# An attention loop's items nine steps deep instead of ten, its group-norm steps turned by half an iteration

## The chip, the core and the metric

The kernel runs on one core of a Trainium2 chip. The metric is device time in microseconds (us) of one execution, on the slowest (here the only) core. The engines are TensorE (PE; its weight loads are shown as PEld), VectorE (DVE), ScalarE (ACT), GpSimd (POOL) and SyncE (SP), which only issues transfers. Each engine takes its own instructions in order, and waits for other engines by semaphores.

## The reference

One encoder block over 1024 tokens of width 1024, in float32. The part that matters here is the middle of it:

```python
h = rms_norm(x, norm_mix_g)
(na_q, na_k, na_v, p_r, p_k, p_v, ..., mem_q, gate_na, gate_rw, gate_mem) = split_columns(h @ w_in)
y_na  = neighborhood_attention(na_q, na_k, na_v, na_rpb)     # 6 heads, windows of 8 x 16 in a 16 x 64 grid
y_rw  = rwkv7_bidirectional(...)                             # two scans, then a group norm per head, x gate
y_mem = memory_attention(mem_q, rms_norm(mem), w_mem_kv)     # 4 heads over 256 memory rows
merged = sigmoid(gate_na) * (y_na @ w_branch_na) + sigmoid(gate_rw) * (y_rw @ w_branch_rw) \
       + sigmoid(gate_mem) * (y_mem @ w_branch_mem)
x = x + merged @ w_out
x = x + expert_choice_ffn(rms_norm(x), ...)                  # 16 experts
```

Both attentions are a softmax over scores times values. The group norm of the scan's output is `((y - mean) * rsqrt(var + eps)) * ln_g + ln_b`, over the 64 channels of a head, plus a bonus, times a gate `sigmoid(lat_g) @ g2`.

## The kernel before

The program is a row of stages: projections and scans, then the **attention stage** (with its tail 843 to 999.6 us of the profiled span), then the merge of the branches, the output projection, the router, and the experts, which take the second half of the span.

The attention stage is an order written out by hand (`tc.manual_schedule()`), a loop over n. It handles 40 items: 24 of the neighbourhood attention (`na_item`, two heads and one eighth of the tokens each) and then 16 of the memory attention (`mem_item`). Each item is cut into parts, and `PIPE` says how many iterations after its start each part is issued, latest part first in an iteration. So iteration n issues lo of item n-9, hi of item n-8, and so on down to score of item n. The parts, with their engines:

- score (PE), top (DVE: bias, maximum), exp (ACT), trans (DVE reciprocal; PE transposes of the probabilities to PSUM tile `tr`), evac (ACT and DVE copy `tr` to `pt`; POOL spreads the reciprocals over `rq`);
- mix (PE: `pt` times values into one half of the PSUM bank `av`, then a transpose of `rq` into the same half), spread (DVE copies that transpose to `rb`), mul (DVE: `av` times `rb` gives `y`), hi (ACT rounds `y` into `yh`), lo (POOL writes the rest to `yl`).

The two halves of `av` take turns, but they are one tile, so mix waits for the last DVE instruction before it that reads `av`. `y` has 3 buffers, `rb` 2.

Between the items runs the group norm (`group_norm`), a generator over 6 tiles of 128 x 512 with 14 steps each. Each iteration from n = 2 on takes two steps: one behind the parts of `PIPE`, and one behind the loads of the next head pair (`side`: `na_load`, `mem_load`, whose steps split q and k into a rounded value and a rest). The steps of one tile, with the lines of the profile of before:

- POOL adds the scans (L876, L877), PE takes off the mean ("cent", L884), ACT copies and squares (L886, L887), PE sums the squares ("hsel", L891), DVE and POOL form the reciprocal root (L210, L211), ACT spreads it (L898), PE transposes it ("pb", L902), DVE multiplies (L904), ACT scales (L906), POOL adds the bonus (L907), PE computes the gate ("pg", L909), DVE multiplies (L913), ACT and POOL write `yh` and `yl` (L916, L917).

All four PE results go through one PSUM tile `gn` with one buffer. When the loop ends, the first weights of the merge (`wraw`, L1127) are loaded over the space of the group norm's tiles.

Of the kernel before, what the change touches and what calls it, by code (L numbers as in the profile page):

```python
# [25 lines left out]
F32 = mybir.dt.float32  # L26
# [4 lines left out]
OP = mybir.AluOpType  # L31
# [22 lines left out]
GN0 = 2  # L54
SCB = 1
WB0, WBK = 2, 4
PIPE = (("lo", 9), ("hi", 8), ("mul", 7), ("spread", 6), ("mix", 5), ("evac", 4), ("trans", 3), ("exp", 2), ("top", 1), ("score", 0))
NB_ = dict(s=2, tr=2, gn=1, av=1)
PSEQ = "E A | B X | x0 | r0 | s0 o0 x1 | r1 | s1 o1 L | | T"
PRI, XTB = None, 3  # L60
# [100 lines left out]
def block_kernel(ctx: ExitStack, tc: tile.TileContext, T, out, dbg=None, upto=99):  # L161
    nc = tc.nc
    dbg = dbg or {}
    V, A, G, PE, SP = nc.vector, nc.scalar, nc.gpsimd, nc.tensor, nc.sync
# [122 lines left out]
    with tc.tile_pool(name="wp", bufs=1, side="right", reuse_waits="tile") as wp:  # L287
# [14 lines left out]
        with (tc.tile_pool(name="qp", bufs=1, side="right", reuse_waits="tile") as qp,  # L302
# [64 lines left out]
            for j in range(3):  # L367
# [13 lines left out]
                for d in range(2):  # L381
# [7 lines left out]
                    rb = qp.tile([128, 8, 2, 64], F32, name="rb", bufs=1)  # L389
# [379 lines left out]

    yctx = ExitStack()  # L770
    ap = yctx.enter_context(tc.tile_pool(name="ap_", bufs=1, side="right", reuse_waits="tile"))
    for nm, w, n in (("sb", 768, 4), ("pt", 768, 2), ("y", 128, 3), ("rb", 128, 2), ("rq", 128, 2)):
        ap.tile([128, w] if w == 128 and nm != "rq" else [128, 2, w // 2], F32, name=nm, bufs=n)
    na, bias = {}, {}
    grid = lambda t: t.rearrange("p (r c) -> p r c", c=64)
# [77 lines left out]
    def group_norm():  # L853
        g2 = gq.tile([128, 384], F32, name="g2")
        SP.dma_start(g2, T["g2"])
        lg = gq.tile([128, S], F32, name="lg")
        SP.dma_start(lg, plat[0])
        its = [(t0, j) for t0 in (0, 512) for j in range(3)]
        ld = {}

        def load(n):
            if n < len(its):
                t0, j = its[n]
                ld[n] = []
                for nm, src in (("y0", yrw[0]), ("y1", yrw[1]), ("b0", bon[0]), ("b1", bon[1])):
                    t = gq.tile([128, 512], F32, name=nm, bufs=2)
                    SP.dma_start(t, src[j][:, t0:t0 + 512])
                    ld[n].append(t)

        load(0)  # L870
        yield
        yield
        for n, (t0, j) in enumerate(its):
            load(n + 1)
            y0, y1, b0, b1 = ld.pop(n)
            G.tensor_tensor(y0, y0, y1, op=OP.add)  # L876
            G.tensor_tensor(b0, b0, b1, op=OP.add)  # L877
            if n == 0:
                A.activation(lg, lg, AF.Tanh, scale=0.5)
                G.tensor_scalar(lg, lg, 0.5, 0.5, op0=OP.mult, op1=OP.add)  # L880
            yield
            yield
            pcb = abank("gn")
            PE.matmul(pcb, C("cent"), y0, start=True, stop=True)  # L884
            yield
            A.activation(y1, pcb, AF.Copy)  # L886
            A.activation(b1, pcb, AF.Square)  # L887
            yield
            pn = abank("gn")
            for i in range(4):  # L890
                PE.matmul(pn[:, 2 * i:2 * i + 2], b1[:, i * 128:(i + 1) * 128], C("hsel"), start=True, stop=True)  # L891
            yield
            rn = gq.tile([128, 8], F32, name="grn", bufs=2)
            rinv_of(pn[:, 0:8], rn, 8, 1.0 / 64, 64e-5)
            rb = gq.tile([128, 8, 64], F32, name="grb", bufs=1)
            yield
            yield
            A.activation(rb, rn[:, :, None].to_broadcast([128, 8, 64]), AF.Copy)  # L898
            yield
            pb = abank("gn")  # L900
            for i in range(4):
                PE.transpose(pb[:, i * 128:(i + 1) * 128], rb[:, 2 * i:2 * i + 2].rearrange("p h t -> p (h t)"), ident)  # L902
            yield
            V.tensor_mul(y1, y1, pb)  # L904
            yield
            A.activation(y1, y1, AF.Identity, bias=P_("lnb", j), scale=P_("lng", j))  # L906
            G.tensor_tensor(y1, y1, b0, op=OP.add)  # L907
            pg = abank("gn")
            PE.matmul(pg, g2[:, j * 128:(j + 1) * 128], lg[:, t0:t0 + 512], start=True, stop=True)  # L909
            yield  # L910
            yield
            yield
            V.tensor_mul(y1, pg, y1)  # L913
            yield
            hi = yh[:, 3 + j, t0:t0 + 512]
            A.activation(hi, y1, AF.Copy)  # L916
            G.tensor_tensor(yl[:, 3 + j, t0:t0 + 512], y1, hi.bitcast(F32), op=OP.subtract)  # L917
# [3 lines left out]
    def attention(sign, score_of, top_of, trans_of, evac_of, mix_of, tokens):  # L921
        o = {}

        def score():
            score_of(o)

        def top():
            o["st"] = ap.tile([128, 8], F32, name="st", bufs=6)
            top_of(o)

        def exp():
            for h in range(2):
                A.activation(o["sb"][h], o["e"][h], AF.Exp, bias=o["st"][:, h:h + 1], scale=sign, accum_out=o["st"][:, 4 + h:5 + h])

        def trans():
            V.reciprocal(o["st"][:, 6:8], o["st"][:, 4:6])
            trans_of(o)

        def evac():
            o["pt"] = ap.tile([128, 2, 384], F32, name="pt", bufs=2)  # L940
            evac_of(o)
            o["rq"] = ap.tile([128, 2, 64], F32, name="rq", bufs=2)
            G.tensor_copy(o["rq"], o["st"][:, 6:8, None].to_broadcast([128, 2, 64]))

        def mix():
            turn[0] ^= 256
            o["av"] = av = avs[:, turn[0]:turn[0] + 256]
            mix_of(o, av)
            PE.transpose(av[:, 128:256], o["rq"].rearrange("p h c -> p (h c)"), ident)

        def spread():
            o["rb"] = rb = ap.tile([128, 128], F32, name="rb", bufs=2)
            V.tensor_copy(rb, o["av"][:, 128:256])

        def mul():
            o["y"] = ap.tile([128, 128], F32, name="y", bufs=3)
            V.tensor_mul(o["y"], o["av"][:, 0:128], o["rb"])

        def hi():
            A.activation(tokens(yh), tokens(o["y"]), AF.Copy)  # L960

        def lo():
            G.tensor_tensor(tokens(yl), tokens(o["y"]), tokens(yh).bitcast(F32), op=OP.subtract)

        return locals()
# [51 lines left out]
    def mem_load():  # L1017
        kv = ap.tile([128, S], F32, name="kt", bufs=1).rearrange("p (j m) -> p j m", j=4)
        SP.dma_start(kv, pkv.rearrange("j p t -> p j t"))
        raw = [ap.tile([128, S], F32, name="q", bufs=2) for _ in range(2)]  # L1020
        for j in range(2):
            SP.dma_start(raw[j], pmq[j])
        yield
        yield
        A.activation(kb[0], kv[:, 0:2], AF.Copy, scale=-1.0)
        V.scalar_tensor_tensor(kb[1], kv[:, 0:2], -1.0, kb[0].bitcast(F32), op0=OP.mult, op1=OP.subtract)
        yield
        yield
        yield
        vm = ap.tile([128, 4, 4, 128], F32, name="VT", bufs=2)[:, 0].rearrange("p (m a) t -> p m (a t)", m=2)  # L1030
        vms.append(vm)
        for j in range(2):
            qm.append([ap.tile([128, 2, 4, 128], F32R, name=f"qb{v}", bufs=2).rearrange("p a g t -> p (a g t)") for v in "hl"])
            for v in (slice(0, 512), slice(512, 1024)):
                A.activation(qm[j][0][:, v], raw[j][:, v], AF.Copy)
                G.tensor_tensor(qm[j][1][:, v], raw[j][:, v], qm[j][0][:, v].bitcast(F32), op=OP.subtract)
                yield
            if j == 0:
                p = abank("s")
                for m in range(2):  # L1040
                    for i in range(2):
                        PE.transpose(p[:, m, i * 128:(i + 1) * 128], kv[:, 2 + i, m * 128:(m + 1) * 128], ident)
                yield p, vm, None
# [37 lines left out]
    with tc.manual_schedule():  # L1081
# [6 lines left out]
        side = {0: na_load(1), 8: na_load(2), 16: mem_load()}  # L1088
        gn = group_norm()
        live, extra, pend = {}, [], []  # L1090
        for n in range(len(items) + 10):
            if n in side:
                extra.append(side[n])
            if n < len(items):
                f, a, b = items[n]
                live[n] = f(a, b)
            for part, lag in PIPE:
                if n - lag in live:
                    live[n - lag][part]()
            for v in pend:  # L1100
                v_out(*v)
            pend = []
            if n >= GN0:
                next(gn, 0)
            live.pop(n - 9, None)
            if n in (4, 8, 12):
                bias_load(n // 4 + 2)
            for g in list(extra):
                v = next(g, 0)
                if v == 0:  # L1110
                    extra.remove(g)
                elif v:
                    pend.append(v)
            if n >= GN0:
                next(gn, 0)
# [456 lines left out]
```

## Time and profile before

| what | us |
|---|---|
| median of 3 runs (2352.61 to 2361.06) | 2359.86 |
| the profiled execution | 2365.62 |
| its span | 2363.8 |
| PE busy in the span | 2238.7 (95%) |
| DVE busy | 1665.0 (70%) |
| ACT busy | 1313.0 (56%) |
| POOL busy | 623.9 (26%) |
| attention stage with its tail, 843 to 999.6 | 156.6 |

The mean granted TensorE clock of the span is 0.973 of full speed. The profiled execution is 5.8 us above the median of the runs, and 1.8 us of it lie outside the span. "Idle before" an instruction is time in which its engine waited, and the arrow names what ended the wait.

### The profile page before, as it was taken

The numbers are of one execution on the slowest core, as the hardware profiler recorded it, in microseconds if no ns is written. First come the engines' busy times: TensorE is split into PE (matmuls) and PEld (weight loads), VectorE is DVE, ScalarE is ACT, GpSimd is POOL, SyncE is SP. The second block draws the span as 40 slices with busy tenths as digits, with TensorE's granted clock in tenths as the row PEclk, the third lists the DMA queues.
The fourth block names the chain that finished last, engine by engine and source line by source line (L and its number), as shares of the span: only waits on it lengthen the run. The fifth ranks groups of instructions, "written<-read, shape, count | busy, mean of one in ns | idle before, by whom it ended". The sixth has DMA issues, their size and how long they took to land.

```text
span 2363.8 us, 33505 instructions
## 1 busy us (share of the span) xinstructions
PE 2238.7 (95%) x12494; PEld 1810.1 (77%) x12494; DVE 1665.0 (70%) x2030; ACT 1313.0 (56%) x1588; POOL 623.9 (26%) x1269
## 2 busy tenths in 40 slices
PE   7999999999999989799948999999999999999996
PEld 6777787877877866577837888888888888888885
DVE  6556566556556246563277888888888988898887
ACT  5554234333334356421226777777777777777775
POOL 1000567567666335442040000000000000000001
PEclk9999999999999999799968999999999999999998
DMA  6435444433433362165396999999999999999994
GB/s 229 157 146 201 123 114 121 138 106 110 128 102 101 116 226 72 59 212 172 121 350 251 378 381 379 391 391 385 393 382 379 380 388 390 389 384 390 380 345 197
DMA packets 196499, 594.19 MB, mean 251 GB/s; under 512 B 53360, under 2 KB 100720, under 8 KB 147184
## 3 DMA queue, kind: packets, MB, share of 16 engines
q1 hardware_dynamic: 189280, 566.20, 64.8%
q0 software_dynamic: 5184, 19.73, 3.0%
q10 hardware_dynamic: 1872, 6.13, 0.7%
q8 instruction: 98, 1.61, 0.3%
q14 instruction: 65, 0.53, 0.1%
HBM read 522.61 MB, written 69.39 MB: 250 GB/s over the span
## 4 chain that ended last, share of the span: by engine, by line
PE 51%; DVE 3%; DMA 1%; ACT 1%; POOL 1%; issue 1%; POOLq 0%; ACTq 0%; DVEq 0%
PE y L1439 14%; PE g L1427 5%; PE g L1428 5%; PE g L1430 5%; PE u L1427 5%; PE u L1428 5%; PE u L1430 5%; PE acc L235 2%; PE acc L237 1%; PE acc L236 1%; PE tr L1487 1%; PE tr L1417 1%; POOL m L1172 1%; PE pl L1259 1%; DVE ye L1345 0%
## 5 line engine op out<-in xcount | busy, mean ns | idle before, releaser
L1404 DVE TENSOR_TENSOR ewl<-raw,ewh 128x2048 fp32r<-128x2048 f32 x380 | 849.8, 2284 | 5.5 <-ACT ewh L1399 5.5
L1399 ACT ACTIVATE ewh<-raw 128x2048 fp32r<-128x2048 f32 x380 | 720.8, 1914 | 112.8 <-PE u L1428 82.3
L1446 POOL DMA_INDIRECT acc<-ye,idx x15 | 43.4, 2891 | 949.2 <-DVE ye L1445 872.2
L728 PE MATMUL acc<-hlo,wh 128*128 128x512 f32 x560 | 226.0, 404 | 0.0
L728 PE MATMUL acc<-hhi,wh 128*128 128x512 f32 x560 | 225.7, 403 | 0.0
L728 PE MATMUL acc<-hhi,wl 128*128 128x512 f32 x560 | 225.4, 402 | 0.0
L568 POOL TENSOR_TENSOR tmul<-tinv,blk 96x60 f32<-96x60 f32 (+24 forms) x496 | 174.1, 351 | 147.1 <-DMA blk<-ldr 109.5
L1427 PE MATMUL g<-ewh,xh 128*128 128x512 f32 x512 | 206.1, 403 | 0.0
L1427 PE MATMUL u<-ewh,xh 128*128 128x512 f32 x512 | 202.2, 395 | 0.0
L1428 PE MATMUL g<-ewh,xl 128*128 128x512 f32 x512 | 200.4, 391 | 0.0
L1428 PE MATMUL u<-ewh,xl 128*128 128x512 f32 x512 | 199.5, 390 | 0.0
L570 POOL TENSOR_TENSOR tinv<-tinv,tmul 96x60 f32<-96x60 f32 (+24 forms) x496 | 176.0, 355 | 38.9
L1439 PE MATMUL y<-ewh,ah 128*128 128x512 f32 x512 | 137.9, 391 | 0.7 <-ACT ah L231 0.7
L1439 PE MATMUL y<-ewl,ah 128*128 128x512 f32 x512 | 137.7, 391 | 0.0
L1439 PE MATMUL y<-ewh,al 128*128 128x512 f32 x512 | 137.7, 391 | 0.0
L1430 PE MATMUL g<-ewl,xh 128*128 128x512 f32 x512 | 137.4, 390 | 0.0
L1430 PE MATMUL u<-ewl,xh 128*128 128x512 f32 x512 | 137.0, 389 | 0.0
L728 PEld LDWEIGHTS acc<-hlo,wh 128*128 128x128 f32 x560 | 106.6, 190 | 20.4
L728 PEld LDWEIGHTS acc<-hhi,wl 128*128 128x128 f32 x560 | 106.2, 190 | 20.5
L728 PEld LDWEIGHTS acc<-hhi,wh 128*128 128x128 f32 x560 | 106.2, 190 | 20.3
L231 ACT ACTIVATE ah<-tr 128x512 fp32r<-128x512 f32 x64 | 38.4, 599 | 143.6 <-PE tr L1487 143.6
L232 DVE TENSOR_TENSOR wl<-wraw,wh 128x1024 fp32r<-128x1024 f32 (+1 forms) x60 | 76.0, 1270 | 57.9 <-ACT wh L231 57.9
(319 smaller groups left out, 4365.9 us busy)
## 6 DMA issues: line engine op xcount, KB each, us to landing
raw<-in_wg_dram SPq DMA_DIRECT2D x128, 1024.0 KB
raw<-in_wu_dram SPq DMA_DIRECT2D x128, 1024.0 KB
raw<-in_wd_dram SPq DMA_DIRECT2D x128, 1024.0 KB
wraw<-in_wt_dram SPq DMA_DIRECT2D x46, 512.0 KB
pt<-pz SPq DMA_DIRECT2D x16, 768.0 KB
pgt<-po SPq DMA_DIRECT2D x48, 256.0 KB
gt<-pgt SPq DMA_DIRECT2D x16, 768.0 KB
blk<-ldr SPq DMA_DIRECT2D x64, 96.0 KB
```

The costliest lines, as they stand in the source:

```text
L232: V.tensor_sub(lo, src, hi.bitcast(F32))
L235: PE.matmul(out_, lh, rh, start=(k_ == 0), stop=False)
L568: G.tensor_tensor(tm[:, 0:m, 0:n], tt[:, 0:m, j:j + 1].to_broadcast([4 * NB, m, n]), lt[:, j, None, j + 1:32].to_broadcast([4 * NB, m, n]) ...
L570: G.tensor_tensor(tt[:, 0:m, j + 1:32], tt[:, 0:m, j + 1:32], tm[:, 0:m, 0:n], op=OP.add)
L728: PE.matmul(p, l[:, k], r[:, k, s0:s0 + 512], start=(k == 0 and i == 0), stop=(k == KD - 1 and i == 2))
L1399: A.activation(hi, raws[seq[n]], AF.Copy)
L1404: V.tensor_sub(lo, raws.pop(seq[n]), his[seq[n]].bitcast(F32))
L1427: PE.matmul(p, xh[:, 4 * b + k], wh[:, k], start=(b == 0 and k == 0), stop=False)
L1428: PE.matmul(p, xl[:, 4 * b + k], wh[:, k], start=False, stop=False)
L1430: PE.matmul(p, xh[:, 4 * b + k], wl[:, k], start=False, stop=(b == 1 and k == 3))
L1439: PE.matmul(py[n], l[:, 2 * b + k], r[:, k, n * 512:(n + 1) * 512], start=(f == 0 and b == 0 and i == 0 and k == 0), stop=(f == 3 and b == ...
L1446: G.indirect_dma_start(out=acc[:, :], out_offset=bass.IndirectOffsetOnAxis(ap=idx[:, e:e + 1], axis=0), in_=ye, in_offset=None, compute_op ...
```

## The change

It has five parts. `spread` and `mul` of an item are issued in one iteration (lag 6 for both, spread first), so that hi and lo come one iteration earlier and the loop has one iteration less. `y` gets 6 buffers and `rb` 3. The group norm starts one step later, so that each of its steps falls into the other half of an iteration. Two of the four subtractions that split the memory attention's q (the second half of each tile) go from POOL to DVE. The items are dropped from the table one iteration earlier.

```diff
-PIPE = (("lo", 9), ("hi", 8), ("mul", 7), ("spread", 6), ("mix", 5), ("evac", 4), ("trans", 3), ("exp", 2), ("top", 1), ("score", 0))
+PIPE = (("lo", 8), ("hi", 7), ("spread", 6), ("mul", 6), ("mix", 5), ("evac", 4), ("trans", 3), ("exp", 2), ("top", 1), ("score", 0))
...
-    for nm, w, n in (("sb", 768, 4), ("pt", 768, 2), ("y", 128, 3), ("rb", 128, 2), ("rq", 128, 2)):
+    for nm, w, n in (("sb", 768, 4), ("pt", 768, 2), ("y", 128, 6), ("rb", 128, 3), ("rq", 128, 2)):
...
         load(0)
         yield
         yield
+        yield
         for n, (t0, j) in enumerate(its):
...
-                G.tensor_tensor(qm[j][1][:, v], raw[j][:, v], qm[j][0][:, v].bitcast(F32), op=OP.subtract)
+                (V if v.start else G).tensor_tensor(qm[j][1][:, v], raw[j][:, v], qm[j][0][:, v].bitcast(F32), op=OP.subtract)
...
-        for n in range(len(items) + 10):
+        for n in range(len(items) + 9):
...
-            live.pop(n - 9, None)
+            live.pop(n - 8, None)
```

Lines from 873 on have a number higher by one in the changed kernel. Three places show what moves.

The first is DVE in the fourth tile of the group norm, while memory items run (L957 mul, L953 spread, L1060 top of a memory item, L904 the group norm's first product). Before:

```order
L957 TENSOR_TENSOR y_10066<-av_8761,rb_10032 128x128 [waits DVE_49,PE_49,Pool_49]
L953 COPY rb_10068<-av_8761 128x128
L936 RECIPROCAL st_10008<-st_10008 128x2 [waits Activation_49]
L1060 TENSOR_REDUCE st_10089<-s_10011 128x2 [waits PE_49,Activation_49]
L904 TENSOR_TENSOR y1_9583<-y1_9583,gn_10099 128x512 [waits PE_49]
L957 TENSOR_TENSOR y_10107<-av_8761,rb_10068 128x128 [waits DVE_49,Pool_49]
L953 COPY rb_10109<-av_8761 128x128
```

And now:

```order
L1061 TENSOR_REDUCE st_10092<-s_10013 128x2 [waits PE_49,Activation_49,Pool_49]
L954 COPY rb_10110<-av_8761 128x128 [waits PE_49]
L958 TENSOR_TENSOR y_10112<-av_8761,rb_10110 128x128 [waits DVE_49]
L1072 COPY pt_10119<-tr_10085 128x2x256 [waits PE_49]
L937 RECIPROCAL st_10053<-st_10053 128x2
L1061 TENSOR_REDUCE st_10131<-s_10095 128x2 [waits PE_49,Pool_49]
L905 TENSOR_TENSOR y1_9587<-y1_9587,gn_10103 128x512 [waits PE_49]
```

The group norm's product stands a whole iteration of DVE work later. mul stands behind spread and reads the `rb` just written, so it waits for DVE itself; its wait for POOL (a free `y`) is gone.

The second is ACT at the second tile's cent (L886, L887 read cent's result; L1002 and L933 are evac and exp of the items, L804 and L810 split k and q). Before:

```order
L804 ACTIVATE KTh<-kt 128x512
L886 ACTIVATE y_8875<-gn 128x512 [waits DMAHW4_49,PE_49]
L887 ACTIVATE b_8879<-gn 128x512 [waits DMAHW6_49,Pool_49]
L960 ACTIVATE yh<-y 128x8x16 [waits DVE_49]
L1002 COPY pt<-tr 96x384 [waits Activation_49]
L933 ACTIVATE sb,st<-sb,st 128x384 [waits DVE_49]
```

And now:

```order
L804 ACTIVATE KTh<-kt 128x512
L961 ACTIVATE yh<-y 128x8x16 [waits DVE_49]
L1003 COPY pt<-tr 96x384 [waits PE_49,Activation_49]
L934 ACTIVATE sb,st<-sb,st 128x384 [waits DVE_49,Pool_49]
L934 ACTIVATE sb,st<-sb,st 128x384
L887 ACTIVATE y_8877<-gn 128x512 [waits DMAHW4_49,PE_49]
L888 ACTIVATE b_8881<-gn 128x512 [waits DMAHW6_49,Pool_49]
```

The two readers of `gn` went behind the next iteration's hi, evac and exp; hsel on PE, which needs the square, kept its iteration.

The third is POOL at the start of the second tile (L917 ends the first tile, L876 and L877 begin the second, L805 is the rest of the next k). Before:

```order
L917 TENSOR_TENSOR yl<-y_8842,yh 128x512 [waits Activation_49]
L876 TENSOR_TENSOR y_8873<-y_8873,y_8875 128x512 [waits DMAHW4_49,DMAHW3_49]
L877 TENSOR_TENSOR b_8877<-b_8877,b_8879 128x512 [waits DMAHW6_49,DMAHW5_49]
L805 TENSOR_TENSOR KTl<-kt,KTh 128x512 [waits DMAHW2_49,Activation_49]
L963 TENSOR_TENSOR yl<-y,yh 128x8x16
```

And now:

```order
L805 TENSOR_TENSOR KTl<-kt,KTh 128x512 [waits DMAHW2_49,Activation_49]
L918 TENSOR_TENSOR yl<-y_8842,yh 128x512 [waits Activation_49]
L877 TENSOR_TENSOR y_8875<-y_8875,y_8877 128x512 [waits DMAHW4_49,DMAHW3_49]
L878 TENSOR_TENSOR b_8879<-b_8879,b_8881 128x512 [waits DMAHW6_49,DMAHW5_49]
L964 TENSOR_TENSOR yl<-y,yh 128x8x16
```

The block of three (L917, L876, L877) now stands behind the split of the next k, which waits for a transfer.

## Rows read from the trace of the kernel before

**Rows 1.** Stretches (us from the span's start): busy per engine, granted clock.
```profile
843.00:999.60 156.60, 131.18 (x1037) 91.10 (x1037) 92.73 (x317) 93.90 (x281) 83.47 (x124) 0.86 0.29 100
963.00:973.00 10.00, 8.40 (x49) 6.01 (x48) 5.00 (x15) 5.65 (x19) 4.08 (x10) 0.51 0.00 1
987.00:1004.00 17.00, 12.36 (x47) 7.99 (x48) 6.79 (x17) 6.06 (x14) 6.25 (x13) 0.50 0.43 144
1004.00:1110.00 106.00, 103.03 (x448) 83.10 (x447) 60.45 (x77) 20.31 (x26) 45.60 (x32) 1.00 0.60 198
```

**Rows 2.** PE's waits, 843 to 978.3: line waited for, total us, times, longest.
```profile
PE av L1007 <- DVE rb L953: 6.2, 10, 1.2
PE av L1076 <- DVE rb L953: 4.6, 5, 1.3
```

**Rows 3.** DVE's waits, 843 to 978.3.
```profile
DVE rinv_t L210 <- PE gn L891: 13.8, 5, 4.9
DVE y L904 <- PE gn L902: 11.7, 5, 4.4
DVE y L957 <- POOL yl L963: 10.1, 7, 3.3
```

**Rows 4.** Timeline at the fourth tile's pb: start, duration, engine, line; idle before.
```profile
944.85 0.66 PE L902 MATMUL gn<-cst,grb 128*128 128x128 f32 x4
...
945.55 0.69 DVE L904 TENSOR_TENSOR y<-y,gn 128x512 f32<-128x512 f32 x1 [0.76 <-PE gn L902]
946.15 0.28 DVE L957 TENSOR_TENSOR y<-av,rb 128x128 f32<-128x128 f32 x1
...
946.35 0.28 DVE L953 COPY rb<-av 128x128 f32<-128x128 f32 x1
...
946.78 0.66 PE L1076 MATMUL av<-pt,VT 128*64 128x128 f32 x8 [1.27 <-DVE rb L953]
```

**Rows 5.** Timeline where the fourth tile ends and the fifth begins.
```profile
951.62 0.69 DVE L1060 TENSOR_REDUCE st<-s 128x2 f32<-128x512 f32 x1
...
952.50 0.64 ACT L916 ACTIVATE yh<-y 128x512 fp32r<-128x512 f32 x1
...
953.21 1.27 POOL L917 TENSOR_TENSOR yl<-y,yh 128x512 fp32r<-128x512 f32 x1 [2.28 <-ACT yh L916]
...
955.76 1.12 PE L884 MATMUL gn<-y,cst 128*128 128x512 f32 x2 [0.45 <-POOL y L876]
...
957.37 0.29 DVE L957 TENSOR_TENSOR y<-av,rb 128x128 f32<-128x128 f32 x1 [1.98 <-POOL yl L963]
...
957.92 0.33 PE L1076 MATMUL av<-pt,VT 128*64 128x128 f32 x2 [1.03 <-DVE rb L953]
```

**Rows 6.** Timeline where the third k is split, beside the second tile's cent.
```profile
878.80 0.63 ACT L804 ACTIVATE KTh<-kt 128x512 fp32r<-128x512 f32 x1 [3.47 <-DMA kt<-pna]
...
881.10 1.95 PE L884 MATMUL gn<-y,cst 128*128 128x512 f32 x2
```

**Rows 7.** Timeline: the last instruction of top beside one of POOL.
```profile
903.96 1.28 POOL L917 TENSOR_TENSOR yl<-y,yh 128x512 fp32r<-128x512 f32 x1 [2.19 <-ACT yh L916]
904.00 1.26 DVE L992 TENSOR_SCALAR st<-st 128x2 f32<-128x2 f32 x1
```

**Rows 8.** Timeline of the tail, the last tile of the group norm.
```profile
986.68 0.63 ACT L898 ACTIVATE grb<-grn 128x512 f32<-128x512 f32 x1 [1.22 <-POOL grn L211]
...
987.64 1.12 PE L1076 MATMUL av<-pt,VT 128*64 128x128 f32 x8 [0.91 <-DVE rb L953]
...
989.82 1.06 PE L902 MATMUL gn<-cst,grb 128*128 128x128 f32 x4
...
993.47 1.92 PE L909 MATMUL gn<-lg,g 128*128 128x512 f32 x2
...
999.57 0.80 PE L235 MATMUL acc<-yh,wh 128*128 128x512 f32 x1 [2.73 <-ACT wh L231]
```

**Rows 9.** SP's waits, 840 to 1005.
```profile
SPq L1127 <- PE gn L909: 38.7, 1, 38.7
```

More of the change, by code (lines that the diff above doesn't have):

```diff
@@ L951, in spread @@
         def spread():
-            o["rb"] = rb = ap.tile([128, 128], F32, name="rb", bufs=2)
+            o["rb"] = rb = ap.tile([128, 128], F32, name="rb", bufs=3)
             V.tensor_copy(rb, o["av"][:, 128:256])
         def mul():
-            o["y"] = ap.tile([128, 128], F32, name="y", bufs=3)
+            o["y"] = ap.tile([128, 128], F32, name="y", bufs=6)
             V.tensor_mul(o["y"], o["av"][:, 0:128], o["rb"])
```

## The prediction

> **What bounds the kernel now.** I first cut the span into stretches [rows 1]. The stage that the change touches is 156.6 us long, 6.6% of the span. PE is busy 131.18 us of it, DVE, ACT and POOL some 83 to 94 us each, so PE is the engine that sets its length, and the reader should look at the 25.4 us in which PE is idle. The second number in that row is the granted clock: 0.86. [...] The stretches 963 to 973 and 987 to 1004 show it at 0.51 and 0.50. The stage after it is PE too: 103.03 of 106 us at full clock, so what the attention stage gives back is not lost in the merge.
>
> Next I asked for what PE waits. Up to 978.3, where the loop runs out of scores, mix waits 6.2 + 4.6 = 10.8 us, 15 times, for DVE's spread [rows 2]. Then for what DVE waits, since it is late: the reciprocal root waits 13.8 us for hsel, the first product 11.7 us for pb, mul 10.1 us for POOL's lo [rows 3]. DVE takes its list in order, so what stands behind such a wait is late: spread, and with it the next mix. The timeline shows it whole at one place [rows 4]: pb ends at 945.51, the product starts at 945.55 and takes 0.69, mul and spread follow, and mix starts at 946.78 after 1.27 us of idle PE. The other kind is where one tile ends and the next begins [rows 5]: POOL works through its three long additions, mul waits 1.98 us for a `y` that lo still reads, and PE's mix waits 1.03 us.
>
> **The change part by part.**
>
> *mul beside spread, six `y`, the half iteration.* All three take away reasons for those 10.8 us. With six `y`, mul needs the lo of four iterations ago and waits for no POOL. With the turn, the reciprocal root and both products are issued behind a whole iteration of DVE's item work, and what they read from PE is an iteration old; nothing of the items stands behind a wait for pb or hsel. What stays: mix still waits for the last reader of `av`. That was spread, starting 0.20 behind mul [rows 4] without reading it. Now it is mul, which needs spread's result: 0.28 for spread, and a hand-off of 0.04 (as from pb's end to the product), so 0.32 instead of 0.20: 0.12 more. With the longer hand-off from DVE to PE (spread ends at 946.63, mix starts at 946.78) it would be 0.23, without any 0.08. DVE has the slack for 40 of these; on PE's path I charge it at the 15 places: 1.8. Term: -10.8 + 1.8 = **-9.0**.
>
> *POOL's three long instructions.* ACT's rounding (L916) needs the second product. That product stood in the iteration before; now it is DVE's last work in the same one, behind top. In rows 5: top ends at 952.31, the product 0.69 later at 953.00, ACT's 0.64 then ends at 953.65 instead of 953.14, and POOL starts at 953.7 instead of 953.21. cent waits for POOL already (0.45), so it comes 0.5 later, at tiles three to six: 2.0. Behind the block stands, after lo, the spreading of `rq`, which the next mix's transpose reads; mul no longer waits, but PE may here. Between nothing and the 1.03 that stood there; I take 0.3, nearer to nothing since PE arrives later too: 1.2. Term: **+3.2**.
>
> *The second tile's start.* Here the block also changes places with the split of the next k, which waits 3.47 us for a transfer [rows 6]. ACT's split ends at 879.43 and the rounding at 880.07; POOL's rest of k (1.27 for this size, as L917) runs to 880.8, the block's first two to 883.3. cent ran at 881.10. The transfer does not come earlier because PE does. Term: **+2.2**.
>
> *hsel, pb, pg.* Each now reads what ACT or DVE issues at the end of the same iteration, where it was the iteration before. PE reaches it after mix, transposes and score, and these cover most of it; without cover one operation of this size is 0.6 to 0.69. 18 places less the tail's three, 0.2 each: **+3.0** (0 to 10).
>
> *The two subtractions on DVE* stand at the end of an iteration, 0.69 each as the product of that size, under PE's work; POOL loses 2.5 us just where its block of the fourth tile is. I take 0. A two-column operation of DVE stood 1.26 us beside POOL's L917 and ended with it [rows 7], so the bound is 2 x 1.3 = 2.6 if a subtraction stands likewise and PE is behind it. [...]
>
> *The tail.* After 978.3 the last tile's chain sets the end: ACT has spread its roots by 987.31, but pb runs at 989.82, since the mix ahead of it started at 987.64 after 0.91 of waiting for a spread that stood behind POOL [rows 8]. pb to the gate's matmul L909 is then 3.65 us, with the product ahead of mul on DVE once more. The first weights of the merge are loaded over the group norm's tiles and wait for L909 [rows 9], and the merge starts at 999.57. Without the waits of mul, pb can follow at about 987.5 to 988 (-2), and mix does not stand behind the product (-1.3, as in rows 4); L909 itself, 1.92 here, takes a little over 1 at full clock (as cent's 1.12), -0.7. Term: **-4.0** (0 to -7; the added step of order in each engine is why not more).
>
> *The clock.* [...] In 963 to 973 it is half of 8.40, 4.2. With the long idle places gone some of the drops will not come; others follow the start of the loop and the wait for k, which stay. Rows give only the bounds, and I take **-3**, somewhat less than one such stretch.
>
> **Sum:** -9.0 + 3.2 + 2.2 + 3.0 + 0 - 4.0 - 3 = -7.6. On the profiled execution 2365.6 becomes 2358.0; that one lies 5.8 above the median of the runs, so the median comes to 2352.
>
> **The rivals.**
>
> [...]
> 2. *The waits change places.* cent waits for POOL and the `rq` transpose takes over what mul waited for, hsel and pg cost 0.4 each, the clock stays as it is: -9 + 5 + 2.2 + 6 - 4 = 0, about 2359. For it: POOL's block is as long as before and only starts later.
> 3. *Slower: ACT as the relay.* ACT's scaling (L906) and rounding (L916) of each tile now wait at the end of ACT's list for a product that DVE issues last in the same iteration, and the next iteration's evac, on which the transposes wait, stands behind. In rows 5 that is 0.5 late and PE does not feel it. 12 places: it eats the gain from 0.6 us of idle PE at each, and the kernel is 0.5% slower from 1.6 us at each, about 2372. Against: evac is needed only after the next mix.
>
> **How the numbers follow.** 0.5%, 11.8 us, is about what a measurement of this kernel can tell from no change; the three runs before spread 8.5 us. I give the forecast 0.40 (2348 to 2356), rival 1 0.30, rival 2 0.20, rival 3 0.10. Faster by over 0.5% is under 2348.1: rival 1 and a tenth of the forecast, 0.34. Slower is rival 3. The rest, 0.56, is within. The range must leave out no more than 0.2: from 2339 (all but a third of rival 1, and with it most of the tail's and the clock's bounds) to 2362 (rival 2 with the subtractions' 2.6); a tenth below and rival 3's tenth above are left out.
>
> **What would show it.** Right: no wait of mul for lo, the reciprocal root and the products without idle before them, mix's wait for DVE (now line 958) under 4 us, L910 before 991 on the old scale, the merge some 4 us sooner after the last score. Wrong: cent (L885) with waits of over 1 us for POOL at each tile, or the `rq` transpose (L950) with waits for POOL of over 3 us in all, or ACT idle before L907 and L917 with PE's transposes behind it. The forecast fails if the granted clock of the stage moves by more than 0.04 either way, or if the tail's chain, one DVE or ACT list longer at each step, is not shorter.

## The result, and the profile after

The changed kernel took 2339.1 us (median of 6 runs, 2337.2 to 2346.7), the kernel before 2354.0 beside it (6 runs, 2352.6 to 2361.1): a ratio of 0.9936, 95% interval 0.9916 to 0.9957, 15 us less, at the lower edge of my range. Two later measurements of the same pair gave 0.9913 (0.9895 to 0.9931) and 0.9922 (0.9901 to 0.9943). The gain is 15 to 20 us, 18 in the mean, where I forecast 7.6. Of the 13 us between the forecast 2352 and 2339.1, some 6 are the start and not the change: the sum began at 2359.86, the median of three runs, and the six runs beside the changed kernel have 2354.0.

The windows view of the stage from its first score to the merge's first matmul, of the changed kernel, with a stretch at its end and the merge behind it:

```profile
839.60:971.90 132.30, 117.88 (x1037) 82.95 (x1037) 96.55 (x318) 93.04 (x281) 81.07 (x122) 0.97 0.34 120
968.00:976.00 8.00, 4.13 (x9) 3.02 (x10) 3.54 (x7) 3.02 (x6) 2.91 (x5) 0.62 0.86 291
971.90:1078.00 106.10, 103.58 (x438) 83.12 (x439) 62.50 (x81) 21.79 (x29) 45.67 (x33) 0.98 0.62 201
```

Against [rows 1], counted from before's first score at 843.1: the stage is 24.2 us shorter in these two executions, and the first part of the merge is not (106.0 us for 436 matmuls before, from 999.6 on, and 106.1 for 438 now). Of that, 10.9 are idle time of PE (25.3 to 14.4). The other 13.3 are its busy time, with the same 1037 instructions: the granted clock of the stage went from 0.86 to 0.97. This pair flatters the change: before's profiled execution (2365.6) lies 11.7 us above the median of its six runs, the changed kernel's (2337.9) 1.2 below. Each kernel was profiled again below.

PE's waits over the whole stage, first before, then changed (line waited for, total us, times, longest):

```profile
PE av L1076 <- DVE rb L953: 8.0, 9, 1.3
PE av L1007 <- DVE rb L953: 6.2, 10, 1.2
PE tr L998 <- ACT pt L1002: 4.8, 3, 3.0
PE acc L235 <- ACT wh L231: 2.7, 1, 2.7
...
PE av L1076 <- ACT b L887: 1.1, 1, 1.1
...
PE gn L884 <- POOL y L876: 0.5, 1, 0.5
```

```profile
PE acc L235 <- ACT wh L231: 4.0, 1, 4.0
PE gn L885 <- POOL y L877: 3.7, 5, 1.6
PE av L1077 <- DVE y L958: 1.7, 3, 1.2
...
PE tr L999 <- ACT pt L1003: 1.3, 1, 1.3
PE av L950 <- POOL rq L944: 1.1, 4, 0.4
...
PE gn L910 <- DVE y L905: 0.6, 2, 0.3
```

These rows close the sum of the idle time: mix for DVE -12.5, the transposes for ACT's evacuation -3.5, mix for ACT -1.1, cent for POOL +3.2, the `rq` transpose +1.1, the gate +0.6, the merge's first weights +1.3: together -10.9.

Cut at the start of the last score, the stage shows where idle and busy time went, before and changed:

```profile
843.10:979.97 136.87, 118.31 (x962) 83.06 (x963) 85.35 (x292) 85.59 (x257) 72.41 (x105) 0.89 0.30 107
979.97:999.57 19.60, 12.83 (x79) 8.00 (x75) 7.32 (x24) 8.17 (x24) 11.06 (x20) 0.68 0.16 54
```

```profile
839.60:956.82 117.22, 108.41 (x961) 76.93 (x963) 89.73 (x298) 85.20 (x259) 69.81 (x104) 0.97 0.35 125
956.82:971.87 15.05, 9.45 (x80) 5.99 (x76) 6.79 (x21) 7.81 (x24) 11.24 (x19) 0.94 0.25 84
```

Up to the last score PE's idle time went from 18.6 to 8.8 us (18.3 in before's second profile, 9.2 and 9.9 in the changed kernel's two others). In the tail behind it the idle time went only from 6.8 to 5.6, and the busy time from 12.8 to 9.4 for the same work; both hold in every profile of the two kernels.

DVE's waits of the changed kernel up to its last score, 839.6 to 957:

```profile
DVE rb L954 <- PE av L950: 10.9, 12, 2.3
...
DVE rinv_t L210 <- PE gn L892: 0.2, 1, 0.2
```

The 35.6 us of [rows 3] have become 0.2: mul no longer waits for lo, nor a product for PE. What DVE waits for now is mix itself: it is early, and PE is what it follows.

The start of the stage, in the timelines of before and changed (start, duration, engine, line, idle before it):

```profile
850.30 1.06 ACT L879 ACTIVATE lg<-lg 128x1024 f32<-128x1024 f32 x1 [2.34 <-DMA lg<-plat]
...
852.29 0.90 PE L998 MATMUL tr<-cst,sb 128*128 128x128 f32 x3 [3.03 <-ACT pt L1002]
```

```profile
844.37 0.61 ACT L804 ACTIVATE KTh<-kt 128x512 fp32r<-128x512 f32 x1
...
845.57 1.06 ACT L880 ACTIVATE lg<-lg 128x1024 f32<-128x1024 f32 x1 [0.59 <-DMA lg<-plat]
...
847.04 0.89 PE L999 MATMUL tr<-cst,sb 128*128 128x128 f32 x3 [1.27 <-ACT pt L1003]
```

The first tile's tanh waits on ACT for the transfer of `lg`, and an evacuation stands behind it. By the turn a split of the next k now stands ahead of the tanh, so ACT works while the transfer runs, and PE waits 1.27 where it waited 3.03. Not all of this is the turn's. The evacuation starts 0.96 us behind the start of the tanh instead of 1.49, which is 0.5; the rest is that `lg` landed 1.2 us sooner after the first score in this execution. In kernels with the turn PE waits 1.27 to 2.69 here, without it 1.79 to 3.03, as the transfer lands. My working does not have this place.

The second tile's start before, where ACT's evacuation stands behind the split that waits 3.47 us for k [rows 6]:

```profile
880.05 0.53 PE L998 MATMUL tr<-cst,sb 128*96 128x128 f32 x3 [1.43 <-ACT pt L1002]
```

And changed, with the place where the fifth tile ends and the sixth begins:

```profile
869.35 0.63 ACT L804 ACTIVATE KTh<-kt 128x512 fp32r<-128x512 f32 x1 [1.52 <-DMA kt<-pna]
...
871.30 1.28 POOL L918 TENSOR_TENSOR yl<-y,yh 128x512 fp32r<-128x512 f32 x1
871.30 1.30 DVE L993 TENSOR_SCALAR st<-st 128x2 f32<-128x2 f32 x1
...
873.86 1.58 PE L885 MATMUL gn<-y,cst 128*128 128x512 f32 x2 [1.61 <-POOL y L877]
...
954.65 0.63 ACT L917 ACTIVATE yh<-y 128x512 fp32r<-128x512 f32 x1 [1.41 <-DVE y L914]
...
955.36 1.27 POOL L918 TENSOR_TENSOR yl<-y,yh 128x512 fp32r<-128x512 f32 x1 [2.75 <-ACT yh L917]
...
956.59 1.27 POOL L877 TENSOR_TENSOR y<-y,y 128x512 f32<-128x512 f32 x1
...
957.92 1.12 PE L885 MATMUL gn<-y,cst 128*128 128x512 f32 x2 [0.81 <-POOL y L877]
```

This is the cost that I had put at +3.2 and +2.2: ACT waits for the product, POOL for ACT, cent for POOL. It is there. But at the second tile cent's new wait of 1.61 stands against the transposes' wait of 1.43, which is gone.

The tail:

```profile
963.31 0.63 ACT L899 ACTIVATE grb<-grn 128x512 f32<-128x512 f32 x1
...
964.16 0.60 PE L903 MATMUL gn<-cst,grb 128*128 128x128 f32 x4
...
965.86 1.12 PE L910 MATMUL gn<-lg,g 128*128 128x512 f32 x2 [0.25 <-DVE y L905]
...
967.01 0.81 SPq L1128 DMA_DIRECT2D wraw<-in_wbr_dram  x2
...
971.19 2.19 ACT L231 ACTIVATE wh<-wraw 128x512 fp32r<-128x512 f32 x4 [1.17 <-POOL yl L918]
...
971.87 0.80 PE L235 MATMUL acc<-yh,wh 128*128 128x512 f32 x1 [4.04 <-ACT wh L231]
```

pb (L903) follows ACT's spreading by 0.22 us after its end, where in [rows 8] 2.5 lay between; the gate's matmul ends at 967.0 and releases SP's transfer. From the start of the last score to the merge it is 15.05 us in all three profiles of the changed kernel, 19.6 and 19.7 in the two of before.

### The profile page after: what moved, and what is told of

Same layout as the page of the kernel before. It is cut to its first block, busy times and chain, and to the rows that moved or that the text cites. A ratio compares the mean times of both kernels' runs of the same rounds, so it can differ in the third digit from the quotient of the medians.

```text
span 2336.1 us, 33479 instructions
## 1 busy us (share of the span) xinstructions
PE 2222.8 (95%) x12494; PEld 1799.1 (77%) x12494; DVE 1668.1 (71%) x2032; ACT 1312.2 (56%) x1588; POOL 619.3 (27%) x1267
## 3 DMA queue, kind: packets, MB, share of 16 engines
q8 instruction: 98, 1.61, 0.3%
## 4 chain that ended last, share of the span: by engine, by line
PE 52%; DVE 3%; DMA 1%; ACT 1%; POOL 1%; issue 1%; POOLq 0%; ACTq 0%; DVEq 0%
PE y L1440 15%; PE g L1428 5%; PE g L1429 5%; PE g L1431 5%; PE u L1428 5%; PE u L1429 5%; PE u L1431 5%; PE acc L235 2%; PE acc L237 1%; PE acc L236 1%; PE tr L1488 1%; PE tr L1418 1%; POOL m L1173 1%; PE pl L1260 1%; DVE ye L1346 0%
```

## The experiments

My theory: DVE's waits for POOL and PE made mix late; the turn and the six `y` remove them together, and with PE's idle places the drops of the clock go. Rivals: one part alone carries it; the clock only differed by chance between two executions. Each time is compared with the kernel before, timed beside it on the same chip; "us" is what the ratio differs from 1, times 2356. Idle, busy and clock are of the profiled execution's stage, first score to merge; "all runs" is the mean of the granted clock over the whole of each timed run. A profile is one execution, and not always a middle one: those of the turn alone and of the gaps are the fastest of their ten runs, those of the changed kernel's second time, without the turn, with three `y` and with the tail the slowest of theirs.

| kernel | ratio (95%) | us | PE idle | PE busy | clock | all runs |
|---|---|---|---|---|---|---|
| before (first profile) | 1 | 0 | 25.3 | 131.2 | 0.86 | 0.976 to 0.978 |
| before again | 0.9997 (0.9982 to 1.0012) | -0.7 | 25.2 | 128.8 | 0.88 | 0.978 |
| changed (first) | 0.9936 (0.9916 to 0.9957) | -15 | 14.4 | 117.9 | 0.97 | 0.980 |
| changed again | 0.9913 (0.9895 to 0.9931) | -20 | 14.8 | 121.8 | 0.93 | 0.981 |
| changed, third time | 0.9922 (0.9901 to 0.9943) | -18 | 15.4 | 118.0 | 0.97 | 0.981 |
| turn alone | 0.9962 (0.9948 to 0.9975) | -9 | 19.3 | 117.0 | 0.97 | 0.979 |
| buffers alone | 0.9988 (0.9976 to 0.9999) | -3 | 22.3 | 124.8 | 0.93 | 0.978 |
| depth alone | 1.0010 (0.9996 to 1.0024) | +2 | 26.0 | 123.4 | 0.94 | 0.977 |
| changed, no turn | 0.9990 (0.9978 to 1.0002) | -2 | 23.9 | 128.4 | 0.89 | 0.978 |
| changed, three `y` | 0.9960 (0.9944 to 0.9976) | -9 | 18.0 | 126.3 | 0.91 | 0.979 |
| changed, old depth | 0.9916 (0.9894 to 0.9938) | -20 | 15.0 | 116.7 | 0.97 | 0.981 |
| changed, subtractions on POOL | 0.9928 (0.9913 to 0.9944) | -17 | 15.5 | 118.1 | 0.96 | 0.981 |
| changed, with gaps | 1.0010 (0.9996 to 1.0024) | +2 | 30.0 | 122.2 | 0.93 | 0.978 |
| changed, additions first | 0.9919 (0.9903 to 0.9935) | -19 | 13.2 | 116.3 | 0.99 | 0.981 |
| changed, tail | 0.9948 (0.9932 to 0.9963) | -12 | 19.1 | 125.4 | 0.89 | 0.979 |
| changed, additions and tail | 0.9911 (0.9894 to 0.9929) | -21 | 11.7 | 119.3 | 0.94 | 0.981 |
| changed, additions and weights | 0.9906 (0.9885 to 0.9927) | -22 | 11.8 | 119.1 | 0.96 | 0.982 |

**The two kernels again.** Before:

> The kernel before, unchanged, profiled once more. If the profiled execution that my sum started from (2365.6) was an unusual one: its stage comes out 147 to 151 us, PE idle in it 24 to 27 us as then, PE's busy time 122 to 126 instead of 131.2 and the granted clock 0.92 to 0.95 instead of 0.86, so that the clock's part of the change is 5 to 8 us and not 13. If it was an ordinary one: 154 to 158 us and 0.85 to 0.88 again.

Changed:

> The changed kernel, unchanged, beside the partial ones on one chip. Expected from its first six runs: 2337 to 2347, median 2339 to 2343, PE idle 14 to 15 us in the stage and the granted clock 0.96 to 0.98.

> The changed kernel once more, beside the two next ones on one chip: 2335 to 2344, median 2338 to 2340.

The windows view of before's and of the changed kernel's second profile:

```profile
838.90:992.90 154.00, 128.82 (x1037) 89.56 (x1037) 92.76 (x316) 93.91 (x281) 83.42 (x124) 0.88 0.29 102
```

```profile
840.30:976.90 136.60, 121.77 (x1036) 86.10 (x1037) 96.21 (x318) 93.06 (x281) 81.16 (x122) 0.93 0.34 116
```

Before's second profile (2358.8 us, the median of its ten runs 2355.4) is at the edge of the second case, so the first was the upper end of an ordinary spread (2350.3 to 2366.1 in all but two of its runs), and not another kind of execution. The changed kernel's second has less clock than I expected (0.93). The idle time is a property of the kernel: 25.3 and 25.2, then 14.4, 14.8 and 15.4. The clock is one only in part: two executions of the changed kernel with the same waits differ by 3.9 us of busy time.

**The parts alone.** The turn:

```diff
         load(0)
         yield
         yield
+        yield
```

> The kernel before with the half iteration's turn alone. My theory: most of DVE's idle time ahead of the reciprocal root (13.8 us) and of the two products (11.7 us) goes, and with it the larger part of PE's waits at mix (10.8 us) and the drops of the clock that follow them; what mul waits for POOL's lo (10.1 us) stays. Stage 140 to 146 us, granted clock 0.91 or more, about 2345. Rival A (the buffers carry the gain): no more than 2 us faster, clock within 0.02 of before. Rival B (the parts only pay together): 2350 to 2356, with mul's wait for POOL grown to over 14 us.

Half of the gain. Mix's waits for DVE fell to 5.7 of 14.2, and DVE's largest wait became mul's for lo, 19.8 us:

```profile
DVE y L958 <- POOL yl L964: 19.8, 10, 4.1
```

Of my theory the waits and the time came out (2348.1, 3 us more than I wrote), with rival B's sign beside them. The stage of the profile (136.3 us, clock 0.97) says less: that execution took 2341.5, 6.6 us under the median of its ten.

The buffers, `("y", 128, 6), ("rb", 128, 3)`:

> The kernel before with six y and three rb alone. My theory: mul's waits for POOL (10.1 us of DVE) go, those for hsel and pb stay and even grow, since they come first in DVE's list; PE's waits at mix fall from 10.8 to 8 or more; about 2351, clock up by no more than 0.04. Rival A (the buffers carry the gain): 2343 or less, PE's waits at mix under 4 us.

The depth, `PIPE = (("lo", 8), ("hi", 7), ("spread", 6), ("mul", 6), ...` and `range(len(items) + 9)`:

> The kernel before with mul in spread's iteration and the loop one shorter, three y and two rb as before. My theory: mul now waits for a lo of the same distance as before, so nothing is gained in the middle, mix pays 0.12 us at some 15 places, and the tail is one iteration (about 1 to 2 us) shorter: 2353 to 2356, clock within 0.03 of before. Rival A (the shorter pipeline carries the tail's gain and the rest): 2348 or less.

With the buffers alone DVE still waits for hsel and pb, 26.5 us in all against 29.2 and 28.0 in before's two profiles, so these waits stayed but did not grow; mix waits for DVE 11.1 us of 14.2, and the clock (0.93) is more than I allowed for:

```profile
DVE rinv_t L210 <- PE gn L891: 14.9, 5, 4.6
DVE y L904 <- PE gn L902: 11.6, 6, 4.3
```

The depth alone gives nothing that the interval tells from zero, though its tail was 16.6 us instead of 19.6: mix's waits for DVE, now for mul, rose from 14.2 to 17.2. -9, -3 and +2 make -10, not -18: turn and buffers need each other.

**One part left out.**

> The changed kernel with the turn of half an iteration taken out. If the turn carries the gain: the reciprocal root and the products of DVE wait for PE again by 20 us or more, PE's waits at mix are back at 9 us or more, the clock 0.95 or less, and the kernel is at 2351 or more. If the buffers with the depth carry it once they are together: 2346 or less.

> The changed kernel with three y and two rb as before. If the six y matter only once the turn is there: mul waits for POOL's lo by 15 us or more of DVE's time, mix waits for mul by 4 us or more in all, about 2346 to 2350, as the turn alone (2348). If POOL's lo comes early enough with the shorter pipeline: 2343 or less, mix's waits under 3 us.

Without the turn next to nothing is left (DVE waits 13.9 us for hsel and 12.3 for pb); without the buffers half. In the run with three `y`:

```profile
DVE y L958 <- POOL yl L964: 12.0, 6, 3.8
```

I had written 15 us or more. Mix waits 3.5 + 3.1 us for mul. When DVE's waits for PE go, its wait for POOL grows: mul's for lo was 14.2 and 14.0 us in before's profiles and 19.8 with the turn alone.

The old depth with all the rest, and the subtractions back on POOL (`G.tensor_tensor(qm[j][1][:, v], ...`):

> The kernel before with the turn, the six y, three rb and the two subtractions on DVE, but mul and lo one iteration later, as before, and the loop one longer. If the shorter pipeline is worth nothing in itself, as alone: within 1.5 us of the changed kernel. If it carries part of the tail: 2 to 4 us slower, with the merge as much later after the last score. If mix's dependence on mul costs what the sum has (1.8 us): 1 to 2 us faster.

> The changed kernel with both second-half subtractions back on POOL. If moving them is worth nothing, as my sum has it: within 2 us of the changed kernel (2339 to 2343). If the move is worth something, since POOL's block of the fourth tile stands at that place: 3 us or more slower, with cent's wait for POOL there over 2 us. [...]

Both within 2.5 us of the changed kernel's measurements, which the intervals do not tell from nothing. So about half of the gain comes with the turn alone and the other half needs the buffers beside it; the depth and the subtractions are worth nothing that these runs can measure. The turn and the buffers without both of the others were not run.

**Idle time put back.**

```diff
+            turn[1] += 1
+            for _ in range(0 if turn[1] % 3 else 6):
+                V.tensor_copy(rb, o["av"][:, 0:128])
             V.tensor_copy(rb, o["av"][:, 128:256])
```

> The changed kernel with six useless copies of 128x128 on DVE (about 0.28 us each, 1.7 us) ahead of spread in every third iteration; the result is the same. If idle places of PE are what lets the clock fall: PE idle in the stage rises from 14.5 by 10 to 20 us, its busy time rises too, from 117.9 to 124 or more with the same 1037 instructions, and the granted clock falls from 0.97 to 0.92 or less; stage 150 us or more. If the clock of the stage does not follow the idle places: idle rises as much, but PE's busy time stays within 2 us of 117.9 and the clock at 0.95 or more; stage 143 to 150.

```profile
838.60:990.80 152.20, 122.21 (x1037) 85.48 (x1037) 118.12 (x396) 94.12 (x281) 81.30 (x122) 0.93 0.31 108
```

Idle rose by 15.6 us and busy time by 4.3, between the two cases that I wrote down. Over its 10 timed runs the clock is 0.978, as before's, where the changed kernel has 0.980 to 0.981. By the ratios the time rose by 17 to 23 us over the changed kernel's three measurements, 2 to 8 more than the idle. So the idle time put back did bring a lower clock; a us of it cost another tenth to half of a us here, and these runs do not say it more closely.

**What the change left: POOL ahead of cent, and the merge's weights.** Additions for the next tile issued ahead of L917 and L918:

```diff
...
+            load(n + 2)
+            if n + 1 < len(its):
+                adds(n + 1)
             hi = yh[:, 3 + j, t0:t0 + 512]
```

> The changed kernel with POOL's two additions for the next tile issued ahead of the rest of the rounding of the tile that ends, the order of nothing else changed. If cent's waits for POOL (3.7 us at five places) are a cost that the turn brought: they fall to under 1 us, and the kernel gains 3 to 5 us on the changed one. If PE only waits elsewhere in the iteration: cent's waits go, others of the same size come, and the time is within 1.5 us of the changed kernel.

cent's waits for POOL go from 3.7 to 0.4, and a part comes up elsewhere: mix waits 3.4 for mul instead of 1.7. Idle is 13.2, some 1.5 less than in the changed kernel, and the time, 2338.1, is the changed kernel's (2337.9 to 2340.4): about half of what was taken from cent is waited for at the next places.

```diff
-GN0 = 2
+GN0 = 1
+        for nm in ("y0", "b1"):
+            gq.tile([128, 512], F32, name=nm, bufs=2)
         g2 = gq.tile([128, 384], F32, name="g2")
...
+        gq.tile([128, 8, 64], F32, name="grb", bufs=1)
+        gq.tile([128, 512], F32, name="b0", bufs=2)
```

> The changed kernel with group norm begun one iteration sooner, and its tiles laid out so that the first weights of the merge are loaded where cent's input was (free some 8 us before the gate's matmul). If the wait for these weights (4.0 us of idle PE, and the clock's fall behind it) sets the tail: the merge starts 3 us or more sooner after the last score, and the kernel gains 3 to 5 us on the changed one. If the last mul and the rounding behind it set it as well: under 1.5 us, PE waiting for ACT's split behind another instruction.

> The changed kernel with both: POOL's additions first, and group norm sooner with its tiles laid out for the merge's weights. If the two gains add up: 6 to 9 us faster than the changed kernel, 2331 to 2335. If one of them only moves a wait: 2336 or more.

The first is slower than the changed kernel, by 3 to 8 us by the ratios. Its merge does start 11.6 us after the last score's start instead of 15.0, as I hoped; but begun one iteration sooner, the first tile's cent waits 5.9 us for POOL, and POOL for a transfer. In the run with both:

```profile
PE gn L894 <- POOL y L876: 4.9, 1, 4.9
```

```profile
POOL y L876 <- DMA y<-yrw: 2.9, 1, 2.9
```

That transfer is no sooner there: POOL's addition, which it releases, starts 7.9 us after the first score in this run and 7.8 in the run with the additions alone, and cent is asked for an iteration sooner. So the start was taken back, and the layout and the additions kept:

> The changed kernel with POOL's additions first and group norm's tiles laid out for the merge's weights, group norm begun where it was. If the first tile's wait (cent 4.9 us for POOL, which waits for the first y transfer) was all that ate the tail's gain in the run with both: that wait is under 1 us, the merge's first matmul waits under 2 us, PE idle in the stage is 8 to 10 us and the time 3 to 5 us under the changed kernel. If the merge's start only waits elsewhere: idle 12 us or more, within 1.5 us of the changed kernel.

```profile
PE acc L235 <- ACT wh L231: 2.8, 1, 2.8
```

```profile
958.53 2.60 SPq L1140 DMA_DIRECT2D wraw<-in_wbr_dram  x2
...
969.28 1.27 POOL L930 TENSOR_TENSOR yl<-y,yh 128x512 fp32r<-128x512 f32 x1 [1.07 <-ACT yh L929]
969.31 2.17 ACT L231 ACTIVATE wh<-wraw 128x512 fp32r<-128x512 f32 x4
```

The weights are now under way 1.4 us after the start of the last score, where it was 10.2, and the merge comes 12.8 us after the last score's start instead of 15.0. What still holds it is ACT, which comes to the split only behind the last rounding. 2336.6 us (2334.9 to 2338.7) against 2340.4 (2337.5 to 2342.2) for the changed kernel on the same chip: the lowest median of all, 3.8 us under the changed kernel, within the 3 to 5 that I expected. The first tile's cent waits 0.3 for POOL, as I wrote; but the merge's first matmul still waits 2.8, not under 2, and the idle went to 11.8, not to 8 to 10.

## Why the prediction was wrong

The cause that the change removes was right: DVE's waits for hsel, pb and lo made mix late, and those waits are gone. The sum was 7 to 12 us too small, and the time went the way of rival 1, which I had estimated at 17 us off, about 2344, with the waits put back covered and 6 of the 17 from the clock; I had held "within 0.5%" for likelier.

**The step that failed is the waits put back on PE.** Up to the last score the sum takes 9.0 off PE's idle time and puts 3.2 + 2.2 + 3.0 = 8.4 back, so that 0.6 is left. Measured, the idle time there fell by 9.1 (means of all profiles, 18.4 to 9.3): most of what I put back did not come, or was set off by waits of ACT that I had not counted. By the terms:

- **mix for DVE, -9.0.** Right, a little low: up to the last score these waits went from 11.3 (10.8 up to 978.3) to 1.4, so -9.9. Of the 1.8 that I put back for mix waiting on mul instead of spread little showed: mix waits 1.7 for mul in the whole stage, and 1.1 for spread in the run with the old depth.
- **POOL's three long instructions, +3.2.** Right: cent waits 1.6 more at tiles three to six and `rq` 1.1 more, so 2.8; 1.0 of it falls behind the last score.
- **The second tile's start, +2.2.** Wrong: cent's new wait is 1.61, but before the transposes waited 1.43 for ACT there (0.72 in before's second profile), since the evacuation stood behind the wait for k. That wait is gone, and 0.2 to 0.9 is left.
- **hsel, pb and pg, +3.0.** Wrong in size: pg 0.6, hsel and pb nothing that the rows show. I charged 0.2 at each of 15 places without a row for it.
- **The start of the stage.** Missing: 1.8 less of waiting for the evacuation in this pair, of which the turn makes 0.5 and the transfer's landing the rest. I followed the turn at the tiles' ends and not at the first tile, where ACT's tanh waits for `lg`.
- **The tail, -4.0.** Measured -4.5, and the steps that I named are there: pb comes 2.5 sooner after the last score (I had 2), from pb to the gate's matmul it is 1.95 less (1.3), that matmul takes 0.8 less (0.7), and the merge starts 0.7 later behind it. What they are made of I had wrong, so the size is partly luck: the tail's idle time fell by 1.2 only, and 3.4 is busy time of the same matmuls at a higher granted clock (0.68 to 0.94), where I had 0.7 for the clock.
- **The subtractions on DVE, 0.** Right within what the runs can tell.
- **The clock, -3.** Not shown wrong. The timed gains of 15 to 20, less 9.1 of idle time and 4.6 in the tail, leave 1 to 6 us for it. The profiles have 7.4 of busy time up to the last score (means 117.1 and 109.8), but both of before's lie above their medians, by 11.7 and 3.4. I chose the 3, somewhat under half of the 8.40 us of 963 to 973 at 0.51; no run shows it as such, nor the 6 for the clock in rival 1's sum. What the runs showed is these 1 to 6 and 3.4 in the tail: the clock's whole share is 5 to 10 us, and my sum had 3.7.

The reason that I gave for little, "the wait for k, which stay", was half right: the drops of the clock at the start, at the second tile and at the merge are there in all three profiles of the changed kernel (lowest granted clock in stretches of 4 us: 0.50 to 0.72 at the start, 0.50 to 0.77 at the second tile, 0.50 to 0.57 at the merge), and a drop at the second tile is missing in before's second (1.00 from 856 to 908). Gone from all three are two that both of before's profiles have: in the first 915 to 922 and 963 to 973 (granted clock 0.53 and, in [rows 1], 0.51), in the second 907 to 915 and 955 to 966 (0.57 and 0.58 in the 4 us from 908 and from 912, 0.50 to 0.68 in the three from 956). The changed kernel there, with 1.00 from 888 to 972 in its two other profiles:

```profile
880.00:964.00 84.00, 78.63 (x727) 56.18 (x724) 63.17 (x202) 60.52 (x191) 52.59 (x84) 1.00 0.17 54
```

Of the signs that I named: no wait of mul for lo, no idle before root and products, mix under 4 us, the gate at 965.86 (969.4 on the old scale, whose first score is 3.5 later), the merge 4.5 sooner, all as forecast. ACT did sit idle before L907 (7.8 us) and L917 (6.1), rival 3's sign, but PE's transposes waited for it once, 1.3 us at the start: the price that rival needed, 1.6 at 12 places, was not there. The stage's clock moved by 0.11 in the first pair and by 0.05 between the two second profiles, which by my own sign made the forecast fail.

What stays open is the clock's exact share: PE's busy time for the same instructions differs by 4 us between executions with equal waits (117.88 and 121.77), why was not shown, and I have two or three profiles of each kernel. By the table, each us of idle time saved went with 1.2 to 2.0 us of time in every kernel that has the turn and no gaps put in.

## What to carry to other kernels

When an engine's list holds two kinds of waits, removing one can let the other come up (here mul's for lo, 14.2 us before and 19.8 with the turn alone): cost them together, and test each part alone and left out before crediting any. A wait that a reordering adds needs a row for its size like one that it removes, and what it takes away elsewhere is to be looked for too. One profile of each kernel does not tell the clock's part: see where each execution lies among the timed runs, and take several. Follow a reordering from its first step, where transfers are still on their way, and not only at the steady places.

## What the runs showed of the hardware

A subtraction on DVE and an addition on POOL, side by side, both with two inputs in SBUF:

```profile
919.18 0.97 DVE L1037 TENSOR_TENSOR qbl<-q,qbh 128x512 fp32r<-128x512 f32 x1 [1.18 <-ACT qbh L1036]
919.56 1.72 POOL L878 TENSOR_TENSOR b<-b,b 128x512 f32<-128x512 f32 x1
```

The other such subtraction takes 0.68. POOL's addition takes 1.26 or 1.27 at four of the six tiles, and 1.80 at 897.73, where another DVE subtraction with two inputs (L1027) ran beside it. DVE's began while POOL's addition before it still ran, and POOL's next began while DVE's ran: 0.29 longer than 0.68, and 0.45 longer than 1.27. PE pays for it once. POOL's spreading of `rq` stands behind that addition, and PE's next transpose waits for it:

```profile
921.97 0.33 PE L950 MATMUL av<-cst,rq 128*128 128x128 f32 x1 [0.37 <-POOL rq L944]
```

In the kernel before, with all four subtractions of q on POOL, the six additions take 1.26 to 1.28. With the subtractions back on POOL that transpose's waits for POOL come to 0.7 us at three places instead of 1.1 at four; the time does not tell the two apart. The two-column L993 at 871.30 above, 0.17 us in the median of its 24, lasted 1.30 beside POOL's L918, as in [rows 7].
